# Hybrid attention/convolution encoder block on one core: the last four query half-blocks are normalised after their load instead of before their store

## The chip, the core and the metric

The kernel runs on one core of a Trainium2 chip. Its engines work side by side, each through a queue of its own: TensorE (PE in the profile, with its weight loads as PEld), VectorE (DVE), ScalarE (ACT), GpSimd (POOL) and SyncE (SP), which here issues all the DMA transfers. The metric is the time of one execution on the device, in microseconds (us).

## What is computed

One encoder layer over a prompt of 256 tokens and a sample of 2048, each with 16 learned tokens in front. The parts that matter here:

```python
proj = rmsnorm(z, norm_w) @ w_in
q, k, v, g_att, c_val, c_glu, g_conv = split(proj)
q = rmsnorm(q.reshape(B, L, 8, 64), q_norm_w)       # each head of 64 by its own root mean square
k = rmsnorm(k.reshape(B, L, 2, 64), k_norm_w)
att = windowed_gqa(q, k, v, sink) * silu(g_att)     # keys within 128 positions, 16 learned keys, a sink
cnv = conformer_conv(c_val, c_glu, ...) * silu(g_conv)
out = z + concat([att, cnv]) @ w_out
```

The change concerns the division of q by its root mean square.

## The kernel before

Everything is float32 in effect: each matmul operand is split into a high and a low part, and three matmuls (high x high, high x low, low x high) stand for one product.

**Projections.** The 18 blocks of 128 tokens are 6 groups of 3, in two halves. The weight columns are 11 units of 256; the last two, units 6 and 7, are the queries: `q_group` makes for each block a tile of 128 tokens x 256 (four heads). The results go through DRAM: `qd` holds the queries of a block, 128 x 512. In the second half these two units come last, and the attention starts under them: `spread`, called after each of the 18 query products, lets a few attention slots run. From its fourth call on, the phase is 2, and a query product is treated as follows. ACT copies it from PSUM to a tile `qr` and squares it; DVE sums the squares; POOL makes `rq`, the reciprocal root (line 186); DVE multiplies `qr` by `rq` (`fin`, in the trace as `qr<-qr,rqq`); and SP stores `qr` to `qd`. `later(k, f)` puts a step off by k ticks. For the last four products (blocks 14 to 17, unit 7, so the second half of their heads) `put_off` is 16, 22, 28 and 34 ticks: their multiplication and store come in the midst of the attention.

**Attention and output.** `slot_step` runs steps of 8 slots. Step `a` makes the scores of block `a` (tiles `S<a>_<kv>_<n>`, DVE adds the bias and takes the maximum at line 550), and the transposed probabilities and the sums `O` of block `a - 1` (`pT_c`, `pT_m`, `pT_x`, split into `ptiles`, line 625). At slot 0 it asks for `load_q(a + 1)`, and at slot 6 `q_prep(a + 1)` transposes it on PE (`qT`). The output projection of pairs of blocks runs in the same slots: `product` accumulates in two PSUM banks `yb0` and `yb1` by a scheme that saves products, with W_out pieces `wo`, `wa` and operand parts in `rest` and `ptiles`. A product need not open its bank: `s3`, then `(0,0)` with rows 6 and 7, go on in the bank of `c1`. `add` (DVE, line 766) adds a finished bank to a tile `yo`, into which `load_x` has loaded the residual rows.

**Order.** PE and POOL run in the order in which the code is written (`manual_schedule`, and `pin` for single instructions elsewhere). DVE, ACT and SP are ordered by a scheduler with a model of the times; each then runs its own list in order. SP's transfers share 8 semaphores in turn, so a transfer is issued when the one eight places ahead of it has landed.

The lines that set the putting off:

```python
tail = max(0, last_n[0] - (LTAGS_N - 4))
put_off = 10 + 6 * tail if tail else 0
rq = head_norm(ps, P, 4, f"q{qi}_{b}", 2 * late + put_off)
```

Of the kernel before, what the change touches and what calls it, by code (L numbers as in the profile page):

```python
# [15 lines left out]
ALU = mybir.AluOpType  # L16
AX = mybir.AxisListType

P = 128
# [10 lines left out]
HD = 64  # L30
# [3 lines left out]
UW = 256  # L34
# [23 lines left out]
VSLOT = 3  # L58
# [77 lines left out]
def blk_local(b):  # L136
    g = b // 3
    return g, (NM if g == 0 else 0) + P * (b % 3)
# [3 lines left out]
def hymba_kernel(  # L142
# [11 lines left out]
    nc = tc.nc  # L154
# [5 lines left out]
    qd = dram.tile([NB, P, 512], F32, name="qd")  # L160
# [35 lines left out]
    def owe(ns):  # L196
        credit[0] -= ns

    def later(k, f):
        due.setdefault(clock[0] + k, []).append(f)  # L200
# [97 lines left out]
    vt, qt, q2t, sbt, pmt, gat, gct, cnt, att, opj = ({} for _ in range(10))  # L298
# [37 lines left out]
    def kind(b):  # L336
        return "first" if b in (0, NB_P) else "last" if b in (NB_P - 1, NB - 1) else "in"

    vt, qt, q2t, sbt, pmt, gat, gct, cnt, att, opj = ({} for _ in range(10))

    def load_k(b):
        t = kw[b % 2].bitcast(F32)
        if kind(b) != "in":
            at = b - (kind(b) == "last")
            for k in range(2):
                nc.sync.dma_start(t[:, :, :, CC + P * k : CC + P * k + P], kd[at + k])
            return
        nc.sync.dma_start(t[:, :, :, CC + QB : RA - QB], kd[b])
        nc.sync.dma_start(t[:, :, :, LA:MA], kd[b - 1][:, :, :, 0:QC])
        nc.sync.dma_start(t[:, :, :, CC : CC + QB], kd[b - 1][:, :, :, QC : QC + QB])  # L350
        nc.sync.dma_start(t[:, :, :, RA - QB : RA], kd[b - 1][:, :, :, QC + QB : P])
        nc.sync.dma_start(t[:, :, :, RA:MB], kd[b + 1][:, :, :, 0:QC])
        nc.sync.dma_start(t[:, :, :, RB:KW], kd[b + 1][:, :, :, QC:P])

    def load_v(b):
        vt[b] = [
            pool["a"].tile([P, KV, P], F32R, tag=f"v{k}", name=f"v{k}_{b}", bufs=VBUFS)
            for k in ("c", "m", "a", "b")[: 4 if kind(b) == "in" else 2]
        ]
        t = [x.rearrange("p a e -> p (a e)").bitcast(F32) for x in vt[b]]  # L360
        if kind(b) != "in":
            at = b - (kind(b) == "last")
            for k in range(2):
                nc.sync.dma_start(t[k], vd[at + k])
            return
        nc.sync.dma_start(t[0][QB:P], vd[b, 0 : P - QB])
        nc.sync.dma_start(t[0][0:QB], vd[b - 1, QC : QC + QB])
        nc.sync.dma_start(t[1][0:QB], vd[b, P - QB : P])
        nc.sync.dma_start(t[1][QB:QC], vd[b - 1, P - QB : P])
        nc.sync.dma_start(t[1][QC:P], vd[b + 1, 0:QC])  # L370
        nc.sync.dma_start(t[2][0:QC], vd[b - 1, 0:QC])
        nc.sync.dma_start(t[2][QC:XR], vmd)
        nc.sync.dma_start(t[3][0:NM], vmd)
        nc.sync.dma_start(t[3][NM:XR], vd[b + 1, QC:P])

    def load_q(b):
        qt[b] = pool["a"].tile([P, 4, P], F32, tag="q", name=f"q{b}")
        nc.sync.dma_start(qt[b].rearrange("p a e -> p (a e)"), qd[b])

    def presplit_wo(e):  # L380

        raw = [sp.tile([P, 2, 400], F32, tag="xt", name=f"wor{e}_{nh}", bufs=XTB)[:, :, :UW] for nh in range(2)]
        for nh in range(2):
            src = w_out[e][:, 512 * nh : 512 * nh + 512].rearrange("p (a n) -> p a n", n=UW)
            nc.sync.dma_start(raw[nh], src)

        def split():
            hi = sp.tile([P, D], F32R, tag="xn", name=f"wohi{e}")
            if e < 4:
                owe(700)  # L390
            to = [wod[PIECES_W.index((e, hl))] for hl in range(2)]
            for nh in range(2):
                part = hi[:, 512 * nh : 512 * nh + 512].rearrange("p (a n) -> p a n", n=UW)
                nc.scalar.copy(part, raw[nh])
                nc.vector.tensor_tensor(raw[nh].bitcast(F32R), raw[nh], part, op=ALU.subtract)
                dst = to[1][:, 512 * nh : 512 * nh + 512].rearrange("p (a n) -> p a n", n=UW)
                later(1, lambda nh=nh, dst=dst: nc.sync.dma_start(dst, raw[nh]))
            later(1, lambda: nc.sync.dma_start(to[0], hi.bitcast(F32)))

        later(2, split)  # L400
# [60 lines left out]
    def load_ga(b):  # L461
        gat[b] = pool["b"].tile([P, 4, P], F32, tag="ga", name=f"ga{b}", bufs=2)
        nc.sync.dma_start(gat[b], gd[0:4, :, P * b : P * b + P].rearrange("j p n -> p j n"))
# [23 lines left out]
    def pin(on):  # L487
        def wrap(f):
            def g(*a, **k):
                r = f(*a, **k)  # L490
                if on:
                    tc.keep_in_program_order(r)
                return r

            return g

        return wrap

    def q_prep(b):
        pt = psum.tile([P, 4, P], F32, tag="b", name=f"qT{b}")  # L500
        for j in range(4):
            pin(b == 0 and j == 0)(nc.tensor.transpose)(pt[:, j, :], qt[b][:, j, :], ident)
        q2 = pool["a"].tile([P, 4, 4, 2, QB], F32R, tag="q2", name=f"q2_{b}")
        q2t[b] = q2
        later(1, lambda: q_split(pt, q2))
# [205 lines left out]
    def with_rest(f):  # L711
        pending.append(f)
        while "rest" in cst and pending:
            pending.pop(0)()
# [102 lines left out]
    def slot_step(s_, slot):  # L817
        a, bb = s_, s_ - 1
        has_a, has_b = a < NB, 0 <= bb < NB
        steps = PLAN if has_b else []  # L820
        if slot == 0:
            if a + 1 < NB:
                load_q(a + 1)
                load_k(a + 1)
        if slot == 1 and has_b and s_ > 1:
            load_ga(bb)
        if slot == VSLOT and 0 < a < NB:
            load_v(a)
        t = 8 * s_ + slot
        with_rest(lambda: None)  # L830
        for f in acts.get(t, ()):
            f()
        if slot < len(steps) and steps[slot]:
            bank(bb, *steps[slot])
        for job in jobs.get(t, ()):
            product(*job)
        if has_a:
            scores(a, slot // 4, slot % 4)
        if slot == (3 if s_ == 1 else 5 if s_ == 3 else QSLOT) and a + 1 < NB:
            q_prep(a + 1)  # L840
        for job in late_jobs.get(t, ()):
            product(*job)
        tick(2400)
# [44 lines left out]
    if True:  # L888
# [300 lines left out]
        def q_group(ws, qi, g, after):  # L1189
            for b in range(3 * g, 3 * g + 3):  # L1190
                ps = proj_te(ws, g, blk_local(b)[1], P)
                late = phase[0] == 2
                raw = None
                tail = max(0, last_n[0] - (LTAGS_N - 4))
                put_off = 10 + 6 * tail if tail else 0
                if late:
                    raw = gp.tile([P, 4, HD], F32, tag="go" if b % 2 else "qs", name=f"qr{qi}_{b}")
                    nc.scalar.copy(raw, ps[:, :UW].rearrange("p (h e) -> p h e", e=HD))
                rq = head_norm(ps, P, 4, f"q{qi}_{b}", 2 * late + put_off)

                def fin(ps=ps, rq=rq, b=b, raw=raw):
                    tag = "go" if phase[0] == 2 and b % 2 else "qs"
                    qs = raw if raw is not None else gp.tile([P, 4, HD], F32, tag=tag, name=f"qs{qi}_{b}")
                    pin(late and not put_off)(nc.vector.tensor_tensor)(
                        qs,
                        qs if raw is not None else ps[:, :UW].rearrange("p (h e) -> p h e", e=HD),
                        rq.unsqueeze(2).to_broadcast([P, 4, HD]),
                        op=ALU.mult,
                    )
                    to = qd[b, :, UW * qi : UW * qi + UW]  # L1210
                    later(2 - late, lambda: nc.sync.dma_start(to, qs.rearrange("p h e -> p (h e)")))

                owe(340)
                later(1 + 2 * late + put_off, fin)
                tick(24 * 110)
                after(b)

# [181 lines left out]
        for i, (c, u, g) in enumerate(items):  # L1399
# [39 lines left out]
            if (c, u) == (0, ORDER[-1]):  # L1439
                p = preps[g + 3]  # L1440
# [85 lines left out]
```

## Time and profile before

| | |
|---|---|
| median of 3 runs | 935.42 us (933.9 to 935.51) |
| profiled execution, time / span | 935.46 us / 933.4 us |
| PE busy | 926.0 us, 99% |
| PE weight loads busy | 877.0 us, 94% |
| DVE / ACT / POOL busy | 786.3 / 447.6 / 350.5 us |
| DMA, mean over the span | 196 GB/s |
| granted TensorE clock | 0.999 |

The span runs from the first to the last instruction; the execution's time is 2.06 us longer. A PE row's end is modelled, and rows overlap, so that PE standing still shows as "idle before" in brackets, or as a later start. Rows of a time line give start, duration, engine, line, operation, tiles out<-in, the count of merged instructions, and in brackets the idle time before and what ended it. SP's rows are the issuing of a transfer, not the transfer.

### The profile page before, as it was taken

How to read it: one execution, taken by the hardware profiler on the slowest of the kernel's cores; microseconds unless marked ns; L12 is line 12 of the kernel's file. 1: busy time of each engine (PE TensorE's matmuls, PEld its weight loads, DVE VectorE, ACT ScalarE, POOL GpSimd, SP SyncE). 2: the span in 40 equal slices, each digit the busy share in tenths (PEclk: the TensorE clock that was granted, in tenths of full speed). 3: DMA queues.
4: the chain of work that ended last, by engine and by line, in shares of the span. 5: the costliest groups of instructions: out<-in, count | busy, mean ns of one | idle time of the engine just before them, and what ended most of it. 6: DMA issues, size and time to landing. Idle time of an engine off the chain costs nothing.

```text
span 933.4 us, 16976 instructions
## 1 busy us (share of the span) xinstructions
PE 926.0 (99%) x5742; PEld 877.0 (94%) x5742; DVE 786.3 (84%) x1380; ACT 447.6 (48%) x1237; POOL 350.5 (38%) x538
## 2 busy tenths in 40 slices
PE   9999999999999999999999999999999999999998
PEld 8999999999999999999999999988888888888887
DVE  5799999989988899999996564689788888887884
ACT  7441222153447750011111356677667676776772
POOL 3420100075675310000000453676664556455652
PEclk9999999999999999999999999999999999999999
DMA  8579685488465472223333688998566566576431
GB/s 299 181 226 360 243 287 186 156 272 311 121 211 176 155 290 91 91 99 110 117 116 116 196 268 265 384 361 251 169 171 187 169 200 167 171 187 190 139 96 47
DMA packets 154183, 182.79 MB, mean 196 GB/s; under 512 B 48784, under 2 KB 114656, under 8 KB 153968
## 3 DMA queue, kind: packets, MB, share of 16 engines
q1 hardware_dynamic: 154096, 181.71, 60.0%
q8 instruction: 45, 0.74, 0.3%
q14 instruction: 42, 0.34, 0.1%
HBM read 115.81 MB, written 65.85 MB: 195 GB/s over the span
## 4 chain that ended last, share of the span: by engine, by line
PE 97%; DVE 1%; ACT 1%; POOL 1%; issue 0%; DVEq 0%; POOLq 0%
PE pj L1050 43%; PE yb L755 20%; PE pj L1066 16%; PE O L644 5%; PE S L490 4%; PE pT_c L610 2%; PE pT_m L610 2%; PE pT_x L610 1%; PE warmup L1291 1%; PE lnu L287 1%; PE lnt L263 1%; PE qT L490 1%; PE xt L1298 0%; DVE xt L959 0%; DVE y L1131 0%
## 5 line engine op out<-in xcount | busy, mean ns | idle before, releaser
L1050 PE MATMUL pj<-xh,ws 128*128 128x384 f32 (+1 forms) x1536 | 395.4, 338 | 0.1
L1131 DVE SCALAR_TENSOR_TENSOR y<-us,cw,y 128x1167 f32<-128x1167 f32 (+2 forms) x258 | 333.5, 1348 | 0.9
L1050 PEld LDWEIGHTS pj<-xh,ws 128*128 128x128 f32 x1536 | 280.9, 188 | 0.4 <-ACT xh L1306 0.4
L1050 PE MATMUL pj<-xl,ws 128*128 128x384 f32 (+1 forms) x768 | 261.4, 341 | 0.2 <-DVE xl L988 0.2
L1066 PE MATMUL pj<-ws,xh 128*128 128x256 f32 (+1 forms) x880 | 165.4, 284 | 0.7 <-ACT sqq L1179 0.4
L1050 PEld LDWEIGHTS pj<-xl,ws 128*128 128x128 f32 x768 | 144.3, 188 | 0.5 <-DVE xl L988 0.5
L1066 PEld LDWEIGHTS pj<-ws,xh 128*128 128x128 f32 (+1 forms) x880 | 136.5, 187 | 1.4 <-issue 1.0
L755 PE MATMUL yb<-wo,rest 128*128 128x512 f32 (+1 forms) x498 | 132.9, 400 | 0.5 <-DVE rest L490 0.5
L1066 PE MATMUL pj<-ws,xl 128*128 128x256 f32 (+1 forms) x440 | 123.8, 281 | 0.0
L755 PEld LDWEIGHTS yb<-wo,rest 128*128 128x128 f32 x498 | 86.8, 189 | 16.0 <-DVE rest L490 0.9
L580 POOL TENSOR_SCALAR sb<-sb,es 128x304 f32<-128x304 f32 (+4 forms) x144 | 73.0, 525 | 58.4 <-PE pT_x L610 20.6
L1165 ACT ACTIVATE go<-pj 128x384 f32<-128x384 f32 x48 | 23.5, 490 | 147.4 <-PE pj L1050 143.2
L185 POOL TENSOR_SCALAR ssk<-ssk 128x2 f32<-128x2 f32 x18 | 11.8, 657 | 208.2 <-ACT sqk L1179 205.2
L562 ACT ACTIVATE sb<-sb,nm 128x304 f32<-128x304 f32 (+4 forms) x144 | 77.2, 536 | 22.1 <-DVE nm L550 20.2
L550 DVE CUSTOM_DVE_ANT_0 sb<-S,bias,vec 128x304 f32<-128x304 f32 (+4 forms) x144 | 73.3, 510 | 11.4 <-PE S L490 10.4
L1066 PEld LDWEIGHTS pj<-ws,xl 128*128 128x128 f32 (+1 forms) x440 | 82.1, 187 | 0.3
L185 POOL TENSOR_SCALAR ssq<-ssq 128x4 f32<-128x4 f32 (+2 forms) x55 | 27.9, 507 | 99.3 <-ACT xn L913 72.8
L490 PEld LDWEIGHTS S<-kw,q 128*128 128x128 f32 x288 | 52.2, 188 | 11.1 <-ACT rest L490 0.3
L490 PE MATMUL S<-kw,q 128*128 128x304 f32 (+4 forms) x288 | 62.3, 299 | 0.0
L755 PE MATMUL yb<-wo,ptiles 128*128 128x512 f32 x216 | 59.9, 407 | 0.0
L490 POOL TENSOR_TENSOR at<-at,ga 128x256 f32<-128x256 f32 x36 | 27.0, 750 | 79.0 <-DVE at L666 79.0
L766 DVE TENSOR_TENSOR yo<-yb,yo 128x512 f32<-128x512 f32 (+1 forms) x55 | 37.1, 674 | 14.7 <-PE yb L755 14.5
(166 smaller groups left out, 1439.7 us busy)
## 6 DMA issues: line engine op xcount, KB each, us to landing
wd<-ws SPq DMA_DIRECT2D x36, 512.0 KB, 5.8
ws<-wd SPq DMA_DIRECT2D x36, 512.0 KB, 6.1
wraw<-in_w_in SPq DMA_DIRECT2D x52, 256.0 KB, 6.3
xn<-in_z SPq DMA_DIRECT2D x18, 512.0 KB, 5.3
gd<-go SPq DMA_DIRECT2D x48, 192.0 KB, 2.9
yo<-in_z SPq DMA_DIRECT2D x36, 256.0 KB, 3.4
wo<-wod SPq DMA_DIRECT2D x18, 512.0 KB, 7.7
out_y<-yo SPq DMA_DIRECT2D x35, 256.0 KB, 2.3
```

The source lines that it names most:

```text
L185: nc.gpsimd.tensor_scalar(src, src, scale, eps, op0=ALU.mult, op1=ALU.add)
L490: r = f(*a, **k)
L550: nc.vector.tensor_tensor_reduce(out=sb[:, n, c0:c1], in0=ps[:, 0:w], in1=cst["bias"][:, kv, at + c0 : at + c1], scale=1.0, scalar=nsnk[:, ...
L562: nc.scalar.activation(sb[:, n, c0:c1], sb[:, n, c0:c1], AF.Exp, bias=nm[:, n : n + 1], scale=-1.0, accum_out=rs[:, n : n + 1],)
L580: nc.gpsimd.tensor_scalar(sb[:, k, a0:a1], sb[:, k, a0:a1], es[:, k : k + 1], 1.0, op0=ALU.mult, op1=ALU.mult)
L610: nc.tensor.transpose(pt[: c1 - c0, n, :], sbt[b, kv][:, n, c0:c1], ident)
L644: nc.tensor.matmul(opj[b, kv][:, n0:n1], t, p, start=(k == "c" and i == 0), stop=(k == "x" and i == len(work) - 1),)
L755: nc.tensor.matmul(ps[:, :n], x[mi][:, i, :], w[wi], start=((name, e) in OPENS and k == 0), stop=(done and e == es[-1] and k == 2), skip_g ...
L766: nc.vector.tensor_tensor(y, ps[:, :n], y, op=ALU.add)
L1050: nc.tensor.matmul(ps[:, :n], ws[:, d, wi, P * half_i : P * half_i + P], x[xi][:, d, o : o + n], start=(k == 0), stop=(k == 3 * ND - 1),)
L1066: nc.tensor.matmul(ps[:rows, :UW], x[xi][:, d, o : o + rows], ws[:, d, wi, :], start=(k == 0), stop=(k == 3 * ND - 1),)
L1131: op = nc.vector.scalar_tensor_tensor(y[:, yo + o0 : yo + o1], u[:, o0 + k : o1 + k], cw[:, j, k : k + 1], y[:, yo + o0 : yo + o1], op0=AL ...
```

## The change

The last four query products are no longer multiplied in `qr`. The raw tile is stored one tick after it is made (`keep`), and its `rq` is kept. When the block's q tile has been loaded, DVE multiplies the half in question in the loaded tile (`scale_q`); the code asks for that at slot 3 of the step before the one that uses it. POOL's work for `rq` stays where it was, 18 to 36 ticks after the product.

```diff
+    raw_q = {}
+
+    def scale_q(b):
+        qi, rq = raw_q[b]
+        q = qt[b].rearrange("p a e -> p (a e)")[:, UW * qi : UW * qi + UW].rearrange("p (h e) -> p h e", e=HD)
+        nc.vector.tensor_tensor(q, q, rq.unsqueeze(2).to_broadcast([P, 4, HD]), op=ALU.mult)
...
         if slot == VSLOT and 0 < a < NB:
             load_v(a)
+        if slot == VSLOT and a + 1 in raw_q:
+            scale_q(a + 1)
...
-                    pin(late and not put_off)(nc.vector.tensor_tensor)(
+                    pin(late)(nc.vector.tensor_tensor)(
...
+                def keep(rq=rq, b=b, raw=raw):
+                    nc.sync.dma_start(qd[b, :, UW * qi : UW * qi + UW], raw.rearrange("p h e -> p (h e)"))
+                    raw_q[b] = (qi, rq)
+
                 owe(340)
-                later(1 + 2 * late + put_off, fin)
+                if put_off:
+                    later(1, keep)
+                else:
+                    later(1 + 2 * late, fin)
```

Lines behind the first insertion stand 7 lower than before (766 is 773, 644 is 651), those behind the second 9 lower. The orders of PE, ACT and POOL are the same before and after. What moves on the others is shown at three places; the numbers at the ends of the names are counts of tiles and differ by a few.

SP, around the last query products, where the residual rows `yo1` of the first pair are loaded. Before:

```order
L457 DMA wo3_6657<-wod_71 128x1024
L474 DMA yo1_6694<-in_z 128x512
L457 DMA wo3_6657<-wod_71 128x1024 x2
L1211 DMA qd_63<-qr1_13_6456 128x256
L378 DMA q4_7037<-qd_63 128x512
L457 DMA wo5_6881<-wod_71 128x1024
L457 DMA wo4_6780<-wod_71 128x1024
L350 DMA kw1_5913<-kd_65 128x4x32
L457 DMA wo4_6780<-wod_71 128x1024 x2
L474 DMA yo2_6695<-in_z 128x512
```

After:

```order
L464 DMA wo3_6660<-wod_71 128x1024 x3
L1223 DMA qd_63<-qr1_15_6577 128x256
L1220 DMA qd_63<-qr1_13_6456 128x256
L1223 DMA qd_63<-qr1_16_6627 128x256
L378 DMA q4_7039<-qd_63 128x512
L464 DMA wo5_6885<-wod_71 128x1024
L464 DMA wo4_6784<-wod_71 128x1024
L1223 DMA qd_63<-qr1_17_6687 128x256
L481 DMA yo1_6698<-in_z 128x512
L350 DMA kw1_5913<-kd_65 128x4x32
L464 DMA wo4_6784<-wod_71 128x1024 x2
L481 DMA yo2_6699<-in_z 128x512
```

The three stores shown (the fourth, of block 14, stands 7 transfers further up) have come in, and the load of `yo1` has moved from between the pieces of `wo3` to behind the first piece of `wo4`. The old places of the four stores were further down, among the loads of the attention's steps 3 to 6.

DVE, where that tile is first added to (`yo1 <- yb0`, the sum `s3`), and PE, where the bank `yb0` is used again by the product (0,0). DVE before:

```order
L625 TENSOR_TENSOR ptiles_6207<-pT1_c_0_6793,ptiles_6207 128x512
L766 TENSOR_TENSOR yo1_6694<-yb0_6725,yo1_6694 128x512
L490 TENSOR_TENSOR rest_6754<-temp1_6768,rest_6754 128x256
L490 TENSOR_TENSOR rest_6754<-cn0_6262,rest_6754 128x256
L490 TENSOR_TENSOR ptiles_6207<-cn0_6262,ptiles_6207 128x256
L666 TENSOR_TENSOR at0_6761<-O0_1_6736,tmp0_1_6858 64x256 x2
```

DVE after, from the same instruction on to the addition:

```order
L632 TENSOR_TENSOR ptiles_6207<-pT1_c_0_6797,ptiles_6207 128x512
L497 TENSOR_TENSOR rest_6758<-temp1_6772,rest_6758 128x256
L497 TENSOR_TENSOR rest_6758<-cn0_6262,rest_6758 128x256
L497 TENSOR_TENSOR ptiles_6207<-cn0_6262,ptiles_6207 128x256
L673 TENSOR_TENSOR at0_6765<-O0_1_6740,tmp0_1_6862 64x256 x2
L632 TENSOR_TENSOR ptiles_6207<-pT1_m_0_6835,ptiles_6207 128x512
L557 ISA sb1_5925,nm2_0_6802<-S2_0_1_6846,bias_5909,vec_77 128x208
L557 ISA nm2_0_6802 128x1
L497 TENSOR_TENSOR rest_6758<-cn1_6258,rest_6758 128x256
L626 SCALAR_TENSOR_TENSOR ptiles_6207<-pT1_x_0_6874,vec_77,ptiles_6207 128x128 x2
L497 TENSOR_TENSOR rest_6758<-at0_6765,rest_6758 128x256
L773 TENSOR_TENSOR yo1_6698<-yb0_6729,yo1_6698 128x512
```

PE at the first half of the product (0,0), with what each instruction waits for. Before:

```order
L644 MATMUL O1_0_6854<-ptiles_6207,vc_1_6633 128x512 x2
L606 MATMUL pT1_x_0_6870<-ident_72,pm1_0_6715 128x128 [waits PE_49,Pool_49]
L755 MATMUL yb0_6725<-wo1_6429,ptiles_6207 128x512 [waits Activation_49]
L755 MATMUL yb0_6725<-wo1_6429,ptiles_6207 128x512
L755 MATMUL yb0_6725<-wo1_6429,ptiles_6207 128x512 [waits DVE_49]
```

After:

```order
L651 MATMUL O1_0_6858<-ptiles_6207,vc_1_6636 128x512 x2
L613 MATMUL pT1_x_0_6874<-ident_72,pm1_0_6719 128x128 [waits PE_49,Pool_49]
L762 MATMUL yb0_6729<-wo1_6429,ptiles_6207 128x512 [waits DVE_49,Activation_49]
L762 MATMUL yb0_6729<-wo1_6429,ptiles_6207 128x512 x2
L762 MATMUL yb0_6729<-wo2_6599,ptiles_6207 128x512 [waits DMAHW6_49]
```

The addition has moved behind ten other instructions of DVE, and the wait for DVE has moved from the product's third matmul to its first.

DVE in step 12, where the multiplication of block 14 has come in. After:

```order
L557 ISA sb0_5921,nm12_0_9188<-S12_0_2_9257,bias_5909,vec_77 128x304
L557 ISA nm12_0_9188 128x1
L385 TENSOR_TENSOR q14_9416<-q14_9416,rqq1_14_6530 128x256
L773 TENSOR_TENSOR yo3_6700<-yb0_6729,yo3_6700 128x512
L557 ISA sb0_5921,nm12_0_9188<-S12_0_3_9287,bias_5909,vec_77 128x304
```

Before:

```order
L550 ISA sb0_5921,nm12_0_9192<-S12_0_2_9261,bias_5909,vec_77 128x304
L550 ISA nm12_0_9192 128x1
L766 TENSOR_TENSOR yo3_6696<-yb0_6725,yo3_6696 128x512
L550 ISA sb0_5921,nm12_0_9192<-S12_0_3_9291,bias_5909,vec_77 128x304
L550 ISA nm12_0_9192 128x1
```

One row is new. It stands in step 12, though the code asks for it in step 13; those of blocks 15, 16 and 17 stand likewise behind S13_0_2, S14_0_2 and S15_0_2. The load of q14 keeps its place on SP.

## The prediction

> **What bounds the kernel now.** First the page, its share of busy time and its chain of work that ended last:
>
> ```profile
> span 933.4 us, 16976 instructions
> PE 926.0 (99%) x5742; PEld 877.0 (94%) x5742; DVE 786.3 (84%) x1380; ACT 447.6 (48%) x1237; POOL 350.5 (38%) x538
> PE 97%; DVE 1%; ACT 1%; POOL 1%; issue 0%; DVEq 0%; POOLq 0%
> ```
>
> TensorE is the chain. Its instructions run in a written order, so whatever makes it stand still is added to the end unless a later wait shrinks. The change touches the stretch behind the last projections (from 606 us) and four steps near 802 to 860 us. The busy times by stretch, cut at the same place of each pair of steps, show what is to be had there:
>
> ```profile
> core 0: us, PE busy (x) PEld busy (x) DVE busy (x) ACT busy (x) POOL busy (x), PEclk, DMA share, GB/s
> 606.00:631.10 25.10, 24.48 (x138) 20.57 (x137) 21.56 (x64) 18.96 (x55) 17.17 (x36) 1.00 1.01 360
> 631.10:674.44 43.34, 43.02 (x238) 36.70 (x238) 37.36 (x99) 30.80 (x83) 29.37 (x47) 1.00 0.72 206
> 674.44:712.18 37.74, 37.69 (x211) 32.13 (x211) 31.39 (x83) 26.36 (x70) 22.25 (x31) 1.00 0.64 175
> 712.18:749.39 37.21, 37.21 (x211) 32.14 (x211) 31.09 (x82) 26.43 (x70) 20.68 (x30) 1.00 0.64 185
> ```
>
> PE idles 0.62 us in the first, 0.32 in the second; the third is 0.53 longer than the fourth with the same 211 matmuls. More than 1.5 us cannot be won here. In the first the DMA engines are full (1.01), in the others not.
>
> **Part 1: four multiplications leave 621 to 676 us.**
>
> ```profile
> L490 DVE TENSOR_TENSOR qr<-qr,rqq 128x256 f32<-128x256 f32 x5 | 2.6, 519 | 0.4 <-POOL rqq L186 0.4
> SPq L1211 <- DVE qr L490: 8.2, 5, 4.6
> ```
>
> The first row is DVE's groups from 600 to 680 us; four of its five are those moved, some 0.43 us each, 1.7 us of DVE. Of PE's waits after this place (0.32 and 0.53) I count 0.7 us as won, between 0 and 0.85. The second row is SP's waits: SP no longer stands at the four late stores. What comes behind them has PE's leave to wait for anyway (K and V tiles), so I count nothing.
>
> **Part 2: four raw stores enter SP's queue near 600 to 613 us.** Nothing of PE waits for a store. But SP issues in order, and the load of `yo1` (the residual rows for the first pair's first sum) drops from a place ahead of four W_out pieces to one behind them and behind all four stores; it stands now where the load of `yo2` stood. The `yo1` load before, the W_out load that is now the last large one ahead of it, and the DMA view of 600 to 620 us:
>
> ```profile
> L474 SPq DMA_DIRECT2D yo<-in_z x1: 907/907/907, 604.2 to 604.2; - x1
> DMA to landing us min/median/max: 7.5/7.5/7.5
> ...
> L457 SPq DMA_DIRECT2D wo<-wod x1: 319/319/319, 609.8 to 609.8; - x1
> DMA to landing us min/median/max: 8.1/8.1/8.1
> ...
> 614.29 0.33 SPq L474 DMA_DIRECT2D yo<-in_z  x1
> ...
> DMA packets 4582, 7.85 MB, mean 393 GB/s; under 512 B 850, under 2 KB 2795, under 8 KB 4580
> ```
>
> `yo1` landed at 604.2 + 7.5 = 611.7. Now the same bytes go ahead of it as ahead of that W_out load (landed 609.8 + 8.1 = 617.9; `yo1` was itself among them), and four stores of 0.131 MB, 0.33 us each at 393 GB/s, 1.3 together. My estimate of its landing is 619.2 us.
>
> What waits for it is DVE's addition `yo1 <- yb0` (line 766), and the order moves that too: from ahead of the low part of `s2` to behind the low part of `at`. The PSUM bank `yb0` is not opened anew for the next product, (0,0) with rows 6 and 7: it goes on in the same bank, so the addition must have read it first. In the order before, PE had that from its earlier wait for `s2`; in the order after, the first matmul of (0,0) itself waits for DVE. The time line before (DVE, ACT and PE rows alone):
>
> ```profile
> 612.41 0.68 DVE L766 TENSOR_TENSOR yo<-yb,yo 128x512 f32<-128x512 f32 x1
> 613.01 0.46 DVE L490 TENSOR_TENSOR rest<-temp,rest 128x256 fp32r<-128x256 f32 x1
> 613.53 1.21 PE L755 MATMUL yb<-wo,rest 128*128 128x512 f32 x4 [0.48 <-DVE rest L490]
> 615.29 1.63 PE L755 MATMUL yb<-wo,ptiles 128*128 128x512 f32 x6
> 616.76 0.41 ACT L490 CAST rest<-at 128x256 fp32r<-128x256 f32 x1
> 616.93 0.59 DVE L619 SCALAR_TENSOR_TENSOR ptiles<-pT_x,vec,ptiles 128x128 fp32r<-128x128 f32 x2
> 617.83 0.61 DVE L490 TENSOR_TENSOR rest<-at,rest 128x256 fp32r<-128x256 f32 x1
> ```
>
> Before, the addition was done at 613.1 and (0,0) started at 615.29. Now it starts when `yo1` is there, 619.2, takes 0.68, and (0,0) starts at 619.95: **4.7 us later**. The PE wait of 0.48 at 613.53 goes (the addition no longer stands ahead of `s2`), but that only lets PE arrive earlier at the new wait. The price from below: even with `yo1` at hand the addition follows line 619 (done at 617.5) and the low part of `at` (0.4), so it ends near 618.5, or 617.9 if DVE keeps the 0.6 us that it gains at 612.41: 2.6 us at least. From above: one more 512 KB load ahead of it (1.3 us at 393 GB/s), 6.0. I take 4.7, since the queue is full throughout by the DMA row.
>
> [...]
>
> **Part 3: four multiplications enter the steady steps.** They are not pinned, so they stand on DVE right behind S12_0_2, S13_0_2, S14_0_2 and S15_0_2, as early as the load of q14 to q17 is thought to be there. DVE holds all that follows until it has landed. SP's order there is unchanged, so the loads of before tell the landings (rows of q14, q15, q16, q17, each with its time to landing):
>
> ```profile
> L378 SPq DMA_DIRECT2D q<-qd x1: 1287/1287/1287, 801.9 to 801.9; - x1
> DMA to landing us min/median/max: 3.6/3.6/3.6
> ...
> L378 SPq DMA_DIRECT2D q<-qd x1: 1605/1605/1605, 819.9 to 819.9; - x1
> DMA to landing us min/median/max: 4.0/4.0/4.0
> ...
> L378 SPq DMA_DIRECT2D q<-qd x1: 430/430/430, 839.9 to 839.9; - x1
> DMA to landing us min/median/max: 4.9/4.9/4.9
> ...
> L378 SPq DMA_DIRECT2D q<-qd x1: 582/582/582, 857.1 to 857.1; - x1
> DMA to landing us min/median/max: 2.9/2.9/2.9
> ```
>
> They land at 805.5, 823.9, 844.8 and 860.0. What DVE did there, and the PE product that needs the low part `pT_c` first:
>
> ```profile
> 802.66 0.08 DVE L550 DVE_READ_ACCUMULATOR2_ANT nm<- 128x1 f32 x1
> 804.05 0.69 DVE L766 TENSOR_TENSOR yo<-yb,yo 128x512 f32<-128x512 f32 x1 [1.31 <-PE yb L755]
> 805.48 0.85 DVE L666 TENSOR_TENSOR at<-O,tmp 64x256 f32<-64x256 f32 x2 [0.28 <-ACT tmp L664]
> 806.36 0.69 DVE L625 TENSOR_TENSOR ptiles<-pT_c,ptiles 128x512 fp32r<-128x512 f32 x1
> 808.84 0.62 PE L644 MATMUL O<-ptiles,vc 128*128 128x512 f32 x2
> ...
> 823.62 0.52 DVE L550 CUSTOM_DVE_ANT_0 sb<-S,bias,vec 128x304 f32<-128x304 f32 x1
> 825.66 0.69 DVE L625 TENSOR_TENSOR ptiles<-pT_c,ptiles 128x512 fp32r<-128x512 f32 x1
> 826.70 0.62 PE L644 MATMUL O<-ptiles,vc 128*128 128x512 f32 x2
> ```
>
> q14: the multiplication ends at 805.5 + 0.43 = 805.9, so the addition of 804.05 is 1.9 late; the idle 0.28 takes a bit, `pT_c` ends at 806.36 + 1.6 + 0.69 = 808.7, and the second matmul of O, which needs it, is due near 809.1. It costs nothing, with 0.4 to spare. q16 is the same place 37.2 us on, with the load 2.1 us later against it (844.8 - 37.2 = 807.6): 2.1 - 0.4 = 1.7 us of PE. q15: 823.9 + 0.43, then 0.42 for the low part of `cn`, so the row of 823.62 starts at 824.75, 1.1 late; `pT_c` ends near 827.35 against 826.9: 0.4. q17 lands 1.1 us earlier in its step than q15 (860.0 - 37.2 = 822.8): 0. The sum is **2.1 us**. From below 0 (all loads as the fastest, 2.9), from above 5.4 (all like q16's 4.9: 0.9 + 1.3 + 1.7 + 1.5).
>
> The multiplication's own 4 x 0.43 us on DVE lies in steps where DVE is busy 31.1 of 37.2 us; the idle 1.31 at 804.05 covers it. PE, ACT and POOL keep their orders word for word.
>
> **Sum.** The profiled execution took 935.46 us, 0.04 from the median of the runs. 935.46 + 4.7 - 0.7 + 2.1 = 941.6 us, 0.65% slower. The ends: 935.46 + 2.6 - 0.85 + 0 = 937.2, and 935.46 + 6.0 - 0 + 5.4 = 946.9.
>
> **Rivals.**
> - *The early stop, cheap (0.17).* `yo1` lands as soon as the page's median for such loads says, 3.4 us after issue, at 617.7; DVE is there no sooner, and only its new place counts: 2.6 to 3.2. For it: the row below. Against it: 7.5 us in the stretch itself. 939.5 to 940.1 with the other terms, 937.4 without part 3.
>
> ```profile
> yo<-in_z SPq DMA_DIRECT2D x36, 256.0 KB, 3.4
> ```
>
> - *The loads of q bind (0.20).* The four land like q16's, part 3 costs 4 to 5.4 us, and the total is near 944 to 945. For it: two of the four took 4 us or more. Against it: the other two.
> - *No slower (0.08).* The new wait of the first (0,0) matmul is for the low part of `cn0` alone, not for the addition, so PE passes as before. Then the addition leaves the way of `s2` (0.48 at 613.53 won) and part 1 wins its 0.7; part 3 at 0 gives 934.3, at 2.1 it gives 936.4. It decides whether the addition reads `yb0` ahead of (0,0): for this rival speaks only that the order names the engine and not the instruction; against it that the wait of before, for just that low part, stood at the third matmul.
>
> **Chances.** The forecast has 0.55, with a range of its own of 940 to 943.5. Runs here tell 0.2% (1.9 us) from no change. Slower takes the forecast, the dear loads and nearly all of the cheap stop, 0.91; of the rest 0.05 is the same and 0.04 faster. The range is 937.6 to 946: below it lies the rival with no stop, above it only both upper ends together.
>
> **What would show it.** Right: a PE idle of 4 us or more ahead of `yb<-wo,ptiles` near 615 us, ended by DVE `yo` of the addition (now line 773), which itself waited for the DMA `yo<-in_z`; that load issued near 614 and landed near 619; DVE waiting 1.5 to 5 us at line 385 for DMA `q`, with PE waiting at O (line 651) about 2 us in all; no wait near 641. Wrong: PE passing (0,0) at 615; DVE finding q14 to q17 landed; or the chain going over DVE between 640 and 800, which would mean that the lateness was not won back by the other engines.

## The result, and the profile after

| | before | after |
|---|---|---|
| median | 934.82 us (933.9 to 935.55, 6 runs) | 942.53 us (941.74 to 944.69, 6 runs) |
| ratio | | 1.0087, 95% interval 1.0073 to 1.01 |
| profiled execution, time / span | 935.46 / 933.4 us | 942.02 / 940.2 us |
| granted TensorE clock, mean | 0.999 | 0.996 |

The change makes the kernel 7.7 us slower by the medians, 6.8 us by the spans of the two profiled executions. The page of the changed kernel, its busy times and the start of its chain of work that ended last:

```profile
span 940.2 us, 16976 instructions
PE 928.9 (99%) x5742; PEld 877.4 (93%) x5742; DVE 785.2 (84%) x1380; ACT 448.0 (48%) x1237; POOL 351.9 (37%) x538
PE 87%; DMA 4%; DVE 4%; issue 1%; ACT 1%; SPq 1%; POOL 1%; DVEq 0%; ACTq 0%; POOLq 0%
```

The chain was 97% PE and is now 87%, with 4% each of DMA and DVE: at some point it leaves PE and goes back over transfers. The largest of PE's waits says where:

```profile
PE yb L762 <- DVE yo L773: 4.5, 1, 4.5
PE O L651 <- DVE ptiles L632: 0.4, 2, 0.2
```

There is one wait of 4.5 us, for the addition `yo1 <- yb0` (now line 773). The time line there (DVE and PE rows; start, duration, and in brackets the idle time before):

```profile
613.67 0.27 PE L613 MATMUL pT_x<-ident,pm 128*128 128x128 f32 x1
...
615.83 0.96 DVE L497 TENSOR_TENSOR rest<-at,rest 128x256 fp32r<-128x256 f32 x1
617.61 0.69 DVE L773 TENSOR_TENSOR yo<-yb,yo 128x512 f32<-128x512 f32 x1 [0.81 <-DMA yo<-in_z]
618.45 2.90 PE L762 MATMUL yb<-wo,ptiles 128*128 128x512 f32 x6 [4.50 <-DVE yo L773]
621.14 0.61 PE L497 MATMUL S<-kw,q 128*128 128x240 f32 x2
621.55 1.07 PE L651 MATMUL O<-ptiles,vm 128*128 128x512 f32 x2
622.42 2.48 PE L762 MATMUL yb<-wo,rest 128*128 128x512 f32 x6
624.74 0.41 PE L497 MATMUL S<-kw,q 128*128 128x272 f32 x2
```

The addition stands behind the low part of `at`, waits another 0.81 us for its load, and PE starts the product (0,0) when it is done. So far this is the forecast. What the forecast did not have is the second number of the PE row: the six matmuls take 2.90 us, where the same six took 1.63 before. The granted clock of this place (the last number but two of a row; PE's busy time is the second):

```profile
617.50:618.00 0.50, 0.00 (x0) 0.00 (x0) 0.39 (x1) 0.00 (x0) 0.42 (x1) 0.59 0.98 389
618.00:624.00 6.00, 5.55 (x14) 4.52 (x15) 0.77 (x3) 0.59 (x2) 2.64 (x4) 0.50 1.05 336
624.00:624.50 0.50, 0.50 (x2) 0.36 (x2) 0.00 (x0) 0.00 (x0) 0.00 (x0) 0.58 0.58 209
624.50:625.00 0.50, 0.50 (x5) 0.45 (x4) 0.06 (x1) 0.00 (x0) 0.00 (x0) 1.00 0.87 193
```

In slices of 0.05 us the clock is 1.00 up to 617.55 and 0.50 from 617.60, 0.50 up to 624.40 and 1.00 from 624.45. The means of 0.59 and 0.58 in the first and the third row put the two steps at 617.59 and 624.42: 6.83 us at half speed, 6.0 of them with PE at work.

To lay out the whole difference I cut both executions at the same instruction, the first transpose `qT` of a block's query tile. For blocks 2 and 3, before and then after:

```profile
601.55 0.60 PE L490 MATMUL qT<-ident,q 128*128 128x128 f32 x4
625.62 0.60 PE L490 MATMUL qT<-ident,q 128*128 128x128 f32 x4
```

```profile
600.39 0.60 PE L497 MATMUL qT<-ident,q 128*128 128x128 f32 x4
631.52 0.60 PE L497 MATMUL qT<-ident,q 128*128 128x128 f32 x4
```

From block 2 to 3 it is 31.13 us instead of 24.07. The stretches from block 3 to 13 and from 13 to 17, each before and then after:

```profile
625.62:811.41 185.79, 185.43 (x1041) 159.25 (x1040) 157.17 (x411) 132.37 (x348) 109.01 (x161) 1.00 0.66 189
811.41:885.75 74.34, 74.34 (x422) 64.26 (x420) 62.24 (x162) 52.77 (x138) 41.39 (x58) 1.00 0.61 173
```

```profile
631.52:816.48 184.96, 184.89 (x1040) 159.24 (x1039) 156.00 (x409) 132.19 (x347) 107.43 (x159) 1.00 0.64 178
816.48:893.01 76.53, 76.08 (x423) 64.36 (x422) 61.41 (x166) 53.17 (x140) 42.99 (x61) 1.00 0.59 169
```

| stretch | difference of the two executions |
|---|---|
| up to block 2, ahead of the changed place | -1.16 |
| block 2 to 3: the stop | +4.32 |
| block 2 to 3: the half clock (7.06 less the stop) | +2.74 |
| block 3 to 13 | -0.83 |
| block 13 to 17 | +2.19 |
| the tail | -0.46 |
| sum | +6.80 |

The stop is 618.45 less 614.13, the time at which (0,0) would have started (615.29 before, less 1.16). The first row is no effect of the change: at block 0 it is there already (569.51 for 570.68 us), and the first early store is issued at 599.24. It is there at 14 us (the four small transposes `xt` start at 12.96 for 14.09 us), behind six transposes that took 1.46 us in the execution of before (from 9.40 us) and 0.87 in the other (from 8.31). The experiments below have block 2 anywhere between 600.3 and 601.9.

### The profile page after: what moved, and what is told of

Read it like the earlier page. It is cut to its first block, busy times and chain, and to the rows that moved or that the text cites. A ratio compares the mean times of both kernels' runs of the same rounds, so it can differ in the third digit from the quotient of the medians.

```text
span 940.2 us, 16976 instructions
## 1 busy us (share of the span) xinstructions
PE 928.9 (99%) x5742; PEld 877.4 (93%) x5742; DVE 785.2 (84%) x1380; ACT 448.0 (48%) x1237; POOL 351.9 (37%) x538
## 4 chain that ended last, share of the span: by engine, by line
PE 87%; DMA 4%; DVE 4%; issue 1%; ACT 1%; SPq 1%; POOL 1%; DVEq 0%; ACTq 0%; POOLq 0%
PE pj L1059 41%; PE yb L762 17%; PE pj L1075 14%; PE O L651 4%; PE S L497 3%; PE pT_c L617 1%; PE pT_m L617 1%; PE pT_x L617 1%; DMA q<-qd 1%; DMA wo<-wod 1%; PE lnt L263 1%; PE lnu L287 1%; DVE xt L968 1%; PE qT L497 1%; DMA wraw<-in_w_in 1%
## 5 line engine op out<-in xcount | busy, mean ns | idle before, releaser
L762 PEld LDWEIGHTS yb<-wo,ptiles 128*128 128x128 f32 x216 | 38.7, 192 | 12.4 <-issue 4.8
```

The source lines that it names most:

```text
L762: nc.tensor.matmul(ps[:, :n], x[mi][:, i, :], w[wi], start=((name, e) in OPENS and k == 0), stop=(done and e == es[-1] and k == 2), skip_g ...
```

## Experiments

My theory after the result: (a) the early stores push the load of `yo1` back on SP, which makes PE stop; (b) the length of the stop halves the clock behind it, 2.7 us; (c) the multiplication on DVE, as early as it stands, waits for the loads of q and holds up what is behind it, 2.2 us. The rivals: the multiplications do most of the harm; the stores' bytes do it, wherever `yo1` stands; the slow matmuls have another cause than the idle time.

**Multiplication moved, stores late.** The store goes back to its old tick:

```diff
-                    later(1, keep)
+                    later(2 + 2 * late + put_off, keep)
```

> The change without its early stores: the raw queries of the last four blocks are stored where the normalised ones were stored before, so that the load of yo1 has its old place in SP's queue; the multiplication on the loaded tile stays as in the changed kernel. My theory (the stores push yo1 back; PE stops 4.5 us for the addition and then runs 6 us at half rate, 2.7 us; and the loads of q cost 2.2): PE starts the product (0,0) with rows 6 and 7 without a stop of over 1 us, the clock stays at 1.00 between 606 and 637 us, and only the waits for q14 to q17 are left: 934.8 + 2.2 - 0.8 = 936.2, between 935.3 and 937.2. Rival (most of the loss comes from the multiplications on DVE or from the other order of DVE, the stop being covered): at least half of the 7.7 us stays, over 938.5.

Measured: 935.87 us (ratio 1.0012, interval 1.0003 to 1.002). The stop and the half clock are gone: (0,0) at its old place, the clock 1.00.

```profile
612.58 0.68 DVE L773 TENSOR_TENSOR yo<-yb,yo 128x512 f32<-128x512 f32 x1
615.43 1.63 PE L762 MATMUL yb<-wo,ptiles 128*128 128x512 f32 x6
```

Block 13 to 17 takes 76.64 us, 2.30 over before, and block 3 to 13 wins 0.56 (811.00 less 625.77 is 185.23): (c) is there alone. The first rival falls.

**Stores early, multiplication where it was.** Beside the early raw store the late multiplication and its store stay, and nothing is multiplied on the loaded tile; the raw bytes are stored as an extra:

```diff
-                    pin(late)(nc.vector.tensor_tensor)(
+                    pin(late and not put_off)(nc.vector.tensor_tensor)(
...
-                    raw_q[b] = (qi, rq)
...
-                else:
-                    later(1 + 2 * late, fin)
+                later(1 + 2 * late + put_off, fin)
```

> The other half alone: the four raw tiles are stored early as in the changed kernel, and beside that the old late multiplications and their stores are kept, with no multiplication on the loaded tiles (so 0.5 MB is stored twice). My theory: the stop of about 4.3 us and the slow 6 us behind it are there as in the changed kernel (7.0 together), nothing waits for q14 to q17, and the 0.8 that DVE won from 621 to 676 us is not: 934.8 + 7.0 = 941.8, between 940.8 and 942.8. Rival (the early stores cost little by themselves, the steady steps cost most): under 938.

Measured: 942.65 us (939.45 to 943.43; ratio 1.0072, 1.0057 to 1.0087). This half brings nearly all of the loss. The excess over 1 of the two halves, 0.0012 and 0.0072, adds up to 0.0084; the whole change has 0.0087. The profiled execution is one of 939.45 us, and it differs from the changed kernel at this place in two things. The first is what the addition waits for:

```profile
616.46 0.97 DVE L497 TENSOR_TENSOR rest<-at,rest 128x256 fp32r<-128x256 f32 x1
617.42 0.69 DVE L773 TENSOR_TENSOR yo<-yb,yo 128x512 f32<-128x512 f32 x1
618.26 2.90 PE L762 MATMUL yb<-wo,ptiles 128*128 128x512 f32 x6 [3.69 <-DVE yo L773]
```

DVE has no idle time ahead of the addition: the load was issued at 612.08 and landed 5.3 us later, at 617.4, while DVE was busy until 617.43. The addition's new place on DVE makes this whole stop; the late load adds nothing to it. The second is the clock:

```profile
618.00:618.50 0.50, 0.24 (x1) 0.27 (x2) 0.12 (x1) 0.00 (x0) 0.50 (x1) 0.64 1.06 420
618.50:621.50 3.00, 3.00 (x9) 2.42 (x10) 0.43 (x1) 0.00 (x0) 2.04 (x5) 0.50 1.11 329
621.50:622.00 0.50, 0.50 (x4) 0.42 (x4) 0.39 (x1) 0.00 (x0) 0.50 (x1) 0.94 1.37 409
```

PE was idle for 3.69 us, and by the same reading the clock was halved from 618.14 to 621.56, 3.42 us, half of the 6.83 above. The six runs fall into two groups: two near 939.5 us with a mean clock of 0.998, four from 942.6 to 943.4 with 0.995 or 0.996. The six of the changed kernel all have 0.996.

**The load of `yo1` first.** The changed kernel, with that one load asked for at rank 8 instead of 12 (the expectation says two ranks; it is four):

```diff
-            (9 + 3 * (p == 0), lambda p=p: load_x(p, (0, 1))),
+            (9 - (p == 0), lambda p=p: load_x(p, (0, 1))),
```

> The changed kernel with all its early stores, but the load of yo1 is asked for two ranks earlier, so that it stands on SP ahead of the W_out pieces and of the stores, as in the kernel before. My theory: it is the place of this one load that costs, not the stores' bytes: no stop over 1 us near 615 us, no slow clock, 936.2 as for the late stores (935.3 to 937.2). Rival (the stores' 0.5 MB in the full stretch from 606 to 618 us delay whatever is loaded there, W_out pieces or yo2 next): a new PE wait of 1 to 3 us between 600 and 640 us, 938 to 940.

Measured: 936.06 us (1.0015, 1.0006 to 1.0023), no stop, the clock 1.00.

```profile
615.39 1.62 PE L762 MATMUL yb<-wo,ptiles 128*128 128x512 f32 x6
```

All early stores are still there: their bytes cost nothing that can be seen, and asking for one load earlier takes 7 us away (block 2 to 3 is 24.04 us for 31.13). With the load early, DVE's addition went back to its old place too. What each does is read from the two stops above. With the addition behind the ten instructions, `stores early alone` lost 3.49 us though DVE did not wait for the load; in the changed kernel the load kept DVE waiting for 0.81 us more, and of its 4.32 us some 3.5 would have stood with the load already there. So most of the stop is DVE's order, and the smaller part the landing itself. The old order alone would hardly have helped, for at its old place the addition would have held DVE until the late load was there; no run tries that. In every kernel here the late load and the late addition go together; that the scheduler moved the addition because it reckoned with the late load is likely, but not shown.

**Extra matmuls in the stop.** To separate the idle time from the delay, `N` matmuls that feed nothing are put on PE right ahead of (0,0), with `N` = 40, 16, 8, 12, 14. They are extra work; the orders of DVE, ACT and POOL around them stay the same:

```diff
+        if (p, name, es) == (0, (0, 0), (6, 7)):
+            fill = psum.tile([P, 512], F32, tag="a", name="fill")
+            for _ in range(N):
+                nc.tensor.matmul(fill[:, :P], ident, ident, start=True, stop=True)
```

> The changed kernel with 40 more matmuls of 128 columns on PE (on the identity, into a bank that nobody reads) right ahead of the product (0,0) with rows 6 and 7, where PE stands idle for 4.5 us. They are extra work and replace nothing. My theory: they lie in the stop (about 2.6 us of the 4.5), the product starts at the same moment as in the changed kernel, and since PE is idle for less than 2 us in one piece the clock stays up; the 2.7 us are saved: 942.5 - 2.7 = 939.8, between 939.2 and 940.5. Rival (the matmuls behind the stop are slow for another reason, the transfers or the operands' weight loads in this stretch): no better than the changed kernel, 942.5, and up to 1 us worse where the extra matmuls delay the product.

Measured with 40: 944.26 us (1.0098, 1.0084 to 1.0113), a miss: I had reckoned 0.064 us for one, an estimate that no run shows, and each showed as two records of 0.113, so that they filled 9.1 us and delayed (0,0) to 622.69. Yet it began 4.2 us later than in the changed kernel and block 3 came only 1.5 us later (32.58 for 31.13); its six matmuls took 1.63 us. So with fewer:

> The changed kernel with 16 extra matmuls of 128 columns ahead of the product (0,0) with rows 6 and 7, in place of the 40 of the run before, which took 9.1 us (80 records of 0.113 us) where the stop had 4.3 to give: there the clock stayed at 1.00 and the product's six matmuls took 1.63 us instead of 2.90, but they began 4.2 us later. 16 take 3.6 us and end near 617.5, about 1 us ahead of the addition. Theory (the idle time in one piece slows the clock, 2.7 us): clock 1.00 behind the stop, 942.5 - 2.7 = 939.8, between 939.3 and 940.5. Rival (the extra matmuls have only moved the loss, for the queue behind them gives it back): 942 or more.

> The same with 8 extra matmuls, 1.8 us, so that the idle time in one piece is 2.5 to 2.7 us. It tells from which length the clock drops. If only a stop near 4 us or longer does it: clock 1.00 and 939.8 as with 16. If any stop of more than some 2 us does it: a slow stretch of 3 to 6 us behind it and 941.5 to 942.5; in between if it depends on when the stop falls.

> The changed kernel with 12 extra matmuls in the stop, between the 8 that left 3.7 us of idle time (clock down, six matmuls in 2.90 us) and the 16 that left 1.1 us (clock 1.00, 1.62 us). They take about 2.8 us, so 2.0 to 2.8 us are left. If the clock drops only after 3 us or more of idle time: six matmuls in 1.63 us, clock 1.00, 939.5 to 941. If 2 us are enough: 2.90 us, and 941.5 to 942.8.

> The same with 14 extra matmuls, which leave 1.4 to 2.2 us. Clock 1.00 and 939.5 to 941 if what was seen at 1.1 us holds here too; a slow stretch and 941.5 or more if the bound lies below 2 us.

The row of the product in each, with 16, 12, 14 and 8 extra matmuls:

```profile
618.61 1.62 PE L766 MATMUL yb<-wo,ptiles 128*128 128x512 f32 x6 [1.07 <-DVE yo L777]
```

```profile
619.33 1.63 PE L766 MATMUL yb<-wo,ptiles 128*128 128x512 f32 x6 [1.68 <-DVE yo L777]
```

```profile
620.83 1.63 PE L766 MATMUL yb<-wo,ptiles 128*128 128x512 f32 x6 [2.29 <-DVE yo L777]
```

```profile
619.41 2.90 PE L766 MATMUL yb<-wo,ptiles 128*128 128x512 f32 x6 [3.73 <-DVE yo L777]
```

The table adds the two executions without extra matmuls, and the one with 40. "Late" is how much later than in before (0,0) starts, both counted from block 2; "rest" is what the stretch from block 2 to 3 has lost beyond that (its length less 24.07, less "late").

| kernel | PE idle in one piece | six matmuls | late | block 2 to 3 | rest |
|---|---|---|---|---|---|
| the change | 4.50 | 2.90 | 4.32 | 31.13 | 2.74 |
| 8 extra | 3.73 | 2.90 | 5.33 | 30.96 | 1.56 |
| stores early alone | 3.69 | 2.90 | 3.49 | 29.06 | 1.50 |
| 14 extra | 2.29 | 1.63 | 5.23 | 29.29 | -0.01 |
| 12 extra | 1.68 | 1.63 | 3.93 | 28.02 | 0.02 |
| 16 extra | 1.07 | 1.62 | 4.46 | 28.53 | 0.00 |
| 40 extra | 0 | 1.63 | 8.49 | 32.58 | 0.02 |

The medians: 8 extra 942.84 us (ratio 1.0088, 1.0074 to 1.0102), 14 extra 943.02 (1.0079, 1.0058 to 1.0101), 12 extra 940.13 (1.0055, 1.004 to 1.007), 16 extra 940.74 (1.0068, 1.0054 to 1.0082). 12 fell into the range that was expected with the clock up; 16 missed it by 0.2 us, 8 lies 0.3 us above the range with the clock down, and 14 has the clock up in its trace but a median like that of a slow stretch.

Extra work in the idle time makes the stretch shorter: with 16, (0,0) started 0.16 us later than in the changed kernel and block 3 came 2.6 us sooner after block 2. Idle pieces up to 2.29 us left the clock at 1.00 and lost nothing but the lateness itself; those of 3.69 us and more halved it and lost 1.5 or 2.7 us besides. In these traces the bound lies between 2.29 and 3.69 us. So (b) is shown, and the rival of another cause falls. The slow stretch is 3.42 us with the stores early alone, 3.41 with 8 extra (by the same reading, from means of 0.91 at 619.00 to 619.50 and 0.68 at 622.50 to 623.00) and 6.83, twice as long, in the changed kernel. What sets these lengths no run here shows.

The times of single kernels are looser than that: with 14 the addition began only at 619.99 in the profiled execution (617.61 in the changed kernel), still waiting for its load. Two of its other three runs (943.42 and 943.61 us), and one of the five with 16 (942.05 us), have a mean clock of 0.998, as the execution with the slow stretch of 3.42 us above; how long PE idled in them is not known. The bound therefore rests on the traced executions alone. The saving in time is clear of the change only with 12, whose interval ends below that of the change; with 16 the two overlap.

**The multiplication on POOL.** The load of `yo1` first, as above, and

```diff
-        nc.vector.tensor_tensor(q, q, rq.unsqueeze(2).to_broadcast([P, 4, HD]), op=ALU.mult)
+        nc.gpsimd.tensor_tensor(q, q, rq.unsqueeze(2).to_broadcast([P, 4, HD]), op=ALU.mult)
```

> The changed kernel with the load of yo1 early on SP, and the four multiplications on the loaded tiles given to POOL instead of DVE. Theory (the q waits cost 2.2 because DVE, with the additions and the low parts behind them, stands still): POOL waits instead, nothing of PE hangs on it there, and with the 0.8 won from 621 to 676 us the time is 934.6 - 0.8 = 933.8, between 933.4 and 934.8. Rival (the multiplication takes longer on POOL and the normalisation of the scores that stands behind it is late): 935.5 to 938.

Measured: 934.72 us (1.0002, 0.9993 to 1.0012), as fast as before. The row of the four (a count, then shortest, median and longest in ns, first and last start), and block 13 to 17:

```profile
L385 POOL TENSOR_TENSOR q<-q,rqq x4: 610/611/612, 819.7 to 877.1; 128x256 f32<-128x256 f32 x4
```

```profile
810.20:884.53 74.33, 74.33 (x423) 64.23 (x420) 61.51 (x162) 52.40 (x138) 43.40 (x62) 1.00 0.62 173
```

They start 14.8 to 16.5 us after DVE's of the kernel with the load of `yo1` first (804.9 to 860.6 there), take 0.61 us each, and the stretch takes 74.33, as before, where the kernel with the load of `yo1` first, with the multiplications on DVE, takes 75.90: (c) is gone. The gain of 0.8 did not come: from block 3 to 13 it won 0.48 (810.20 less 624.89 is 185.31), and block 2 to 3 lost 0.28 (24.35 for 24.07).

**The multiplication later on DVE.** The load of `yo1` first, and the multiplication pinned at slot 5:

```diff
-        if slot == VSLOT and a + 1 in raw_q:
+        if slot == QSLOT - 1 and a + 1 in raw_q:
...
-        nc.vector.tensor_tensor(
+        pin(True)(nc.vector.tensor_tensor)(
```

> The changed kernel with the load of yo1 early on SP, and the four multiplications on DVE two places of the plan later and held there (slot 5 instead of 3, some 4 us later, one place ahead of the transposes that use the tile). Theory (DVE stands 9.1 us for loads of q that land 1.4 to 2.5 us after it gets there): the loads have landed by then, no wait for q on DVE, 933.8, between 933.4 and 934.9; the transposes may have to wait for DVE if its queue is long there, which is the rival: 0.3 to 0.8 us in each of the four steps, 935.5 to 937.

Measured: 934.6 us (1.0, 0.9992 to 1.0009). DVE no longer waits for q:

```profile
L497 DVE TENSOR_TENSOR q<-q,rqq 128x256 f32<-128x256 f32 x4 | 2.3, 564 | 0.0
```

```profile
L385 DVE TENSOR_TENSOR q<-q,rqq x4: 426/428/618, 810.5 to 867.0; 128x256 f32<-128x256 f32 x4
...
  DMA q<-qd: 10.9, 4
```

The first row is this kernel's, the others are the changed kernel's, where DVE stood 10.9 us in four pieces. Block 13 to 17 takes 74.82 us, 0.48 over before, in two steps of 0.23 and 0.25; what makes these is open. Neither of the two last kernels beats the kernel before: with its side effects taken away the change is worth nothing that can be told within these intervals of about 0.1% either way.

## Why the prediction was right

It said 941.6 us, 937.6 to 946, slower with 0.91; measured 942.53. Direction, places and waits were right, one term was missing, and the largest was split wrongly between its two causes. That the two numbers lie so close is in part luck: in the two profiled executions the terms of the change add up to 8.42 us (4.32, 2.74, -0.83 and 2.19), where 6.1 were forecast. The medians are 7.7 apart, and the forecast started from 935.46, 0.64 above the median of the six runs.

- **The stop, 4.7 us: 4.32.** It stands at the forecast row, ended by the forecast addition. `yo1` was issued at 612.31 and landed at 617.51; put back by the 1.16 us of offset that is 613.5 and 618.7 against the 614 and 619.2 of the estimate. But the landing was not what made most of it. Part 2 lets the landing set the time and counts 2.6 us for DVE's new order alone; here DVE was done with the low part of `at` only at 616.79 (it took 0.96 us, where 0.4 was counted), so that a load already there would have left 3.5 us, and in the kernel with the early stores alone 3.49 us stood without any wait for the load. The landing added 0.8. The rival "early stop, cheap" had this cause right (only the new place counts) and its price, 2.6 to 3.2, too low.
- **The half clock, not in the sum: 2.74.** The step that failed is Part 2, which charged the stop with its length only; the runs showed that matmuls behind a stop of 3.7 us or more take 2.90 us for 1.63, and that filling the stop takes the term away. It is the main reason why the median lies above the forecast. The range held it only through room left for other things, a later landing and dearer loads of q.
- **Four multiplications gone, -0.7: -0.83,** with -0.56 where the stores are late. The kernel with the early stores alone, which kept these multiplications in their place, has -0.19 there too (815.69 less 630.09 is 185.60). Right within what two executions tell.
- **The waits for q, 2.1: 2.19, but not where I put them.** Each lies between two transposes (q14 is multiplied at 810.46, between those of blocks 12 and 13); these steps lost 0 (q14, as forecast), 0.73 (q15, 0.4 forecast), 0.46 (q16, 1.7) and 0.76 (q17, 0); another 0.24 fell in a step without a multiplication. The loads took 2.8, 2.9, 4.3 and 2.8 us to land. For q16 that is less than the 4.9 before; for q15 the multiplication took 0.62 us instead of 0.43. That the sum fits is chance: the errors cancel, and the kernels with the late stores and with the load of `yo1` first, which have the same multiplications, lost 2.30 and 1.56.
- **"No slower"** needed PE to pass (0,0); the wait names the addition. **"The loads of q bind"** needed landings like 4.9 us; the longest was 4.3.
- No wait near 641, as said: PE is busy for 184.89 of 184.96 us from block 3 to 13. Nothing but the 0.83 of the lateness was won back there, since PE is the chain.

## What to carry to other kernels

The early stores cost by what they pushed back, not by their bytes: look for the next load whose reader PE waits for, and ask for it first. Then look at the order of the engine that reads it: here the reader had moved behind ten instructions, and that alone made 3.5 of the 4.3 us. When a forecast makes PE stand still in one piece for longer than the 2.3 us that were harmless here, add the slow matmuls behind it to the price, which the three traced stops of 3.7 us and more all had: 1.5 us (slow for some 3.4 us) or 2.7 (slow for 6.83). An instruction that may wait for a transfer belongs on the engine, or at the place of the queue, behind which nobody on the chain is waiting.

## What was unexpected of the hardware

The granted clock had two values around the stop, 1.00 and 0.50, and the slow stretch lasted 3.42 us in one execution and 6.83 in another, for stops of 3.69 and 4.50 us; one kernel's runs fell into two groups whose mean clocks, 0.998 and 0.996, match a stretch of 3.42 us and one of 6.83. The groups are 3 us apart, though, and the longer stretch costs only some 1.2 us more by the table (2.74 less 1.50); the rest of the distance is not explained. On POOL the multiplication of 128x256 took 0.61 us, against 0.42 at best on DVE, where it reached 0.92 in one place of the kernel with the load of `yo1` first.
